# Halved convolution operations, re-timed norm broadcasts and an end that accumulates onto the old sum, in a hybrid decoder step

## The chip, the core and the metric

The kernel runs on one core of one Trainium2 chip. The metric is the device time of one execution in microseconds (us). The core's engines are named as the profile names them: PE (TensorE, matrix products), PEld (its weight loads), DVE (VectorE), ACT (ScalarE), POOL (GpSimd) and SP (SyncE, which here only issues transfers). Matrix products write into PSUM, a small memory of eight banks; everything else that is on the chip lies in SBUF. Each engine works through its own queue in order, and waits on semaphores for the others.

## The reference

One inference step of a one-layer hybrid decoder: sliding-window attention and a state-space mixer side by side, then a squared-ReLU MLP and a last norm. 1024 prompt tokens (plus 16 meta tokens) and 32 sample tokens go through it in fp32. What matters here:

```python
def causal_conv(x, prev, conv_w, conv_b):
    t = x.shape[1]
    xp = jnp.concatenate([prev, x], axis=1)
    y = sum((xp[:, j:j + t] * conv_w[j] for j in range(CONV_W)), conv_b)      # CONV_W = 4
    return jax.nn.silu(y), xp[:, t:]

def rmsnorm(x, g):
    xf = x.astype(jnp.float32)
    y = xf * lax.rsqrt(jnp.mean(xf * xf, axis=-1, keepdims=True) + EPS)
    return (y * g.astype(jnp.float32)).astype(x.dtype)

def mix_and_mlp(h, ao, so, attn_out_g, w_out, norm2_g, w_up, w_down):
    mix = jnp.concatenate([rmsnorm(ao, attn_out_g), so], axis=-1)             # ao: attention's output
    h = h + mix @ w_out
    u = jax.nn.relu(rmsnorm(h, norm2_g) @ w_up)
    return h + (u * u) @ w_down
...
    y_prompt = rmsnorm(hp, norm_f_g)[:, N_META:]
    y_sample = rmsnorm(hs, norm_f_g)
```

## The kernel before

Channels lie on the 128 partitions and tokens along the free axis. Each fp32 product is done as three matrix products of a high and a low part (`three`, or `whi`, `wlo`, `acth`, `actl` in the names). All matrix products but the transposes are issued by the helper `mm` at line 202, so the profile gives them line 202 and only their tiles tell them apart.

**Attention and convolution** (about 100 to 300 us into the span). `interleave` walks through slots. The generator `projections` gives one slot per input projection: 24 matrix products into a bank `g`, 304 or 384 columns wide. At the head of each slot every live chain is advanced by one step. The chains are nine attention tiles, of which tile i (1 to 8) starts in slot 24 + round(3.3 (i - 1)), that is 24, 27, 31, 34, 37, 40, 44, 47. Counted from its start S, a tile (`attn_block`) prepares its operands `kS` and `Qs` in slot S, makes scores (bank `s`) and the softmax `p` in S+1 and S+2, transposes `p` into banks `pt` (line 743) and copies them out as `pT` (line 745) in S+3 and S+4, and multiplies by the values (bank `o`) in S+5. `norm_o` then norms the tile: squares `sqo`, their sum over channels by a matrix product `o<-ones,sqo` in S+7, the root `rsb` (DVE line 320, then POOL line 321), a diagonal `dg` (ACT line 376), a broadcast by the matrix product `pt<-dg,ones`, and a multiplication (DVE, line 762) that reads the bank. There are two `pt` buffers. The broadcast stands in slot S+9 for tiles 1 to 7, since `late` is true for them, and in S+8 for tiles 0 and 8.

The convolution (`conv`) runs under the same slots, one group m of 128 channels after the other: ACT makes the first tap (line 522), DVE the other three (line 524, each 128x1096 in and out of the same tile `acc`, named `xs` or `bc`), ACT a tanh (line 529), DVE the last product (line 531). POOL shares the stage: it splits weights (`wlo`, line 234) and scales the softmax (`p`, line 733). The order of the instructions within a queue is set when the program is built, by a scheduler that may move them past each other, so the code's order alone does not tell it.

**The end.** The output has four parts of TQ = 264 tokens. The last loop (`last`) adds one more product to part 0 (16 steps of four channel groups), then to groups 0, 1 and 2 of part 1 (16 steps), then to group 3 of part 1 (16 steps). After each group DVE adds the bank to `h` (line 1801). `final_last` is the norm of part 1. It sums the squares of seven groups ahead, while group 3 is still being multiplied (`c<-ones,ac`), then squares group 3 (line 1756), sums it over channels for three token tiles, takes the root (lines 1762 and 1763), builds three diagonals (line 1654), broadcasts (`c<-dg,ones`), multiplies `h` on DVE in four pieces (line 1665), and stores each (line 1768), on SP's and ACT's queues in turn. Six idle products into a bank `g` keep PE busy while the root is taken.

Of the kernel before, what the change touches and what calls it, by code (L numbers as in the profile page):

```python
# [15 lines left out]
D = 1024  # L16
# [152 lines left out]
_OUTS = [('y', (128, 4, 8, TQ)), ('kp', (128, 128)), ('vp', (128, 128)), ('cv_', (128, 8, 27)), ('hp', (128, 512)),  # L169
# [22 lines left out]
def body(ctx: ExitStack, tc: tile.TileContext, xT, xm, win, wdt, wo, wu, wd, ck, cv, sc, st, sT, vec, consts,  # L192
# [323 lines left out]
    def conv(m, cb):  # L516
        acc = (xs if m < 4 else bc[0])[:, m % 4, :]
        cw_ = lambda j: vec[:, V_CW + 8 * j + m:V_CW + 8 * j + m + 1]
        seq = cb[:, 0:56].rearrange("p (b t) -> p b t", t=7)
# [3 lines left out]
        for j in range(1, 4):  # L523
            DVE.scalar_tensor_tensor(out=acc, in0=cb[:, j:j + CL], scalar=cw_(j), in1=acc, op0=ALU.mult, op1=ALU.add)  # L524
            if j > 1:
                yield
# [4 lines left out]
        DVE.scalar_tensor_tensor(out=acc, in0=th, scalar=1.0, in1=acc, op0=ALU.add, op1=ALU.mult)  # L531
# [223 lines left out]

    def norm_o(i, o_ps=None):
# [4 lines left out]
        ps = yield from rms_bcast(pa, POOL, ps_tile, sq[:, :, :rows], rows, 512, "o", "pt", late=0 < i < NT - 1)  # L761
# [106 lines left out]
    for q in range(4):  # L868
# [16 lines left out]
               [(24 + round(3.3 * (i - 1)), attn_block(i)) for i in range(1, NT)])  # L885
# [731 lines left out]
    sums2 = {}  # L1617

    def squared(c, n):

        hc = h[:, n:n + 4, two(c)]
        q2 = hpool.tile([128, 4, TQ], F32, name="q2", tag="q2", bufs=2)
# [7 lines left out]
        else:  # L1630
            sums2[c] = hpool.tile([128, TQ], F32, name=f"ac{c}")
# [7 lines left out]
    def gained(c, m):  # L1639
        hm = h[:, m, two(c)]  # L1640
        ACT.activation(out=hm, in_=hm, func=AF.Copy, scale=vec[:, V_GF + m:V_GF + m + 1])

    AT = (0, 128, TQ - 128)

    def sum_tokens(tag, acc):
        pt = bank(tag)
        for q, a in enumerate(AT):
            mm(pt[:, q:q + 1], acc[:, a:a + 128], ones[:, 0:1], True, True)
        return pt
# [7 lines left out]
    def spread(tag, dgs):  # L1657
        ps = bank(tag)
        for a, dg in zip(AT, dgs):
# [3 lines left out]
    def normed(c, ps, m, n):  # L1663
        hm = h[:, m:m + n, two(c)]
        DVE.tensor_tensor(out=hm, in0=hm, in1=ps[:, :TQ].unsqueeze(1).broadcast_to([128, n, TQ]), op=ALU.mult)

    def final(c, tag, waits):

        yield from squared(c, 0)
        pt = sum_tokens(tag, sums2[c])  # L1670
# [33 lines left out]
    for i, (j, k) in enumerate(down):  # L1704
# [32 lines left out]
    kept2 = [w2p.tile([128, 2, TQ], F32R, name=f"tk{k}") for k in range(16)]  # L1737

    def final_last():

        hc = h[:, :, two(1)]
        q2 = hpool.tile([128, 4, TQ], F32, name="q2", tag="q2", bufs=2)
# [7 lines left out]
        pt = sum_tokens("c", sums2[1])  # L1750
# [3 lines left out]
        DVE.tensor_scalar(out=part, in0=pt[:, 0:3], scalar1=1.0 / D, scalar2=EPS, op0=ALU.mult, op1=ALU.add)  # L1754
        yield
        ACT.activation(out=q2[:, 3], in_=hc[:, 3], func=AF.Square)
        pt = sum_tokens("c", q2[:, 3])
# [3 lines left out]
        rs = hpool.tile([128, 3], F32, name="rs3", tag="rs3", bufs=2)  # L1761
        DVE.scalar_tensor_tensor(out=rs, in0=pt[:, 0:3], scalar=1.0 / D, in1=part, op0=ALU.mult, op1=ALU.add)
        POOL.tensor_tensor(out=rs, in0=rs, in1=nhalf[:, 0:3], op=ALU.pow)
        gained(1, 3)
        ps = spread("c", [diag(rs, q) for q in range(3)])
# [65 lines left out]
```

## Time and profile before

| what | value |
|---|---|
| median of 3 runs | 1129.44 us (1129.01 to 1130.55) |
| the profiled execution's own time | 1129.86 us |
| its span, from the first to the last instruction | 1128.1 us |
| what lies around the span | 1.76 us |
| busy in the span: PE, PEld | 1110.9 us (98%), 1072.0 us (95%) |
| busy in the span: DVE, ACT, POOL | 838.4 us (74%), 569.9 us (51%), 220.8 us (20%) |
| granted TensorE clock | 0.999 |

A busy PE is not a PE at its peak: matrix products are pipelined, and the ends of them are modelled. The shares are averages over stages with different limits, so each part of the change is to be judged in its own stage.

### The profile page before, as it was taken

To read this page: it belongs to the slowest core of one execution; us is meant where nothing else is said; L and a number is where in the kernel's file an instruction comes from. 1 tells how busy PE (TensorE), PEld (TensorE's weight loads), DVE (VectorE), ACT (ScalarE), POOL (GpSimd) and SP (SyncE) were. 2 spreads that over 40 slices of the span, in tenths; PEclk is the share of its full clock that TensorE was granted. 3 is DMA by queue.
4 is the path that set the end of the run, shared out by engine and by line. 5 is a ranking of instruction groups with operands and counts; after the bars stand their busy time and mean duration, and the time that the engine had idled before them with its cause. 6 is when DMAs were issued, how large, how long until landed. Compare 5 with 4: busy or idle time off the path is not lost.

```text
span 1128.1 us, 21788 instructions
## 1 busy us (share of the span) xinstructions
PE 1110.9 (98%) x8405; PEld 1072.0 (95%) x8405; DVE 838.4 (74%) x1627; ACT 569.9 (51%) x1203; POOL 220.8 (20%) x290
## 2 busy tenths in 40 slices
PE   9999999999999999999999999999999999999997
PEld 8989989889888899999999999999999999999996
DVE  6646888885788968998877767766599656778483
ACT  8312467575666648854444444444434334546461
POOL 0442365664343442210000000000000000000010
PEclk9999999999999999999999999999999999999999
DMA  8131110111466476666652433525989653465272
GB/s 291 66 98 38 38 27 31 38 53 42 157 199 211 130 273 211 214 184 224 208 187 106 168 147 134 180 89 182 383 302 321 192 174 102 125 199 163 77 237 99
DMA packets 84424, 177.64 MB, mean 157 GB/s; under 512 B 10692, under 2 KB 32740, under 8 KB 82272
## 3 DMA queue, kind: packets, MB, share of 16 engines
q1 hardware_dynamic: 77392, 141.58, 40.3%
q0 software_dynamic: 6224, 33.74, 7.5%
q8 instruction: 66, 1.08, 0.4%
q10 hardware_dynamic: 704, 0.93, 0.2%
q14 instruction: 38, 0.31, 0.1%
HBM read 125.49 MB, written 50.72 MB: 156 GB/s over the span
## 4 chain that ended last, share of the span: by engine, by line
PE 80%; DVE 9%; ACT 5%; issue 3%; DMA 2%; POOL 0%; POOLq 0%; DVEq 0%; ACTq 0%
PE g L202 43%; PE b L202 19%; PE c L202 9%; PE s L202 3%; PE o L202 1%; ACT p L679 1%; PE y L202 1%; DMA wdr<-in_wd 1%; PE pt L743 1%; DVE Qs L710 1%; DVE bc L524 1%; DVE Sd L1600 1%; DVE p L677 1%; ACT acth L407 1%; PE pt L202 1%
## 5 line engine op out<-in xcount | busy, mean ns | idle before, releaser
L202 PE MATMUL g<-acth,whi 128*128 128x384 f32 (+2 forms) x528 | 161.8, 331 | 0.2 <-DVE qT L454 0.2
L202 PE MATMUL g<-acth,wlo 128*128 128x384 f32 (+2 forms) x528 | 159.4, 327 | 0.4 <-DVE hb L985 0.4
L202 PE MATMUL g<-actl,whi 128*128 128x384 f32 (+2 forms) x432 | 140.6, 326 | 0.0
L1613 ACT CAST ts<-tr 128x528 fp32r<-128x528 f32 x92 | 58.3, 634 | 118.7 <-PE b L202 100.1
L1614 DVE TENSOR_TENSOR ts<-tr,ts 128x528 fp32r<-128x528 f32 x92 | 65.1, 708 | 53.1 <-ACT ts L1613 52.7
L202 PEld LDWEIGHTS g<-acth,whi 128*128 128x128 f32 x528 | 97.2, 188 | 2.0 <-issue 1.0
L202 PEld LDWEIGHTS g<-acth,wlo 128*128 128x128 f32 x528 | 97.1, 188 | 0.9 <-DVE hb L985 0.6
L202 PEld LDWEIGHTS g<-actl,whi 128*128 128x128 f32 x432 | 81.4, 188 | 0.1
L321 POOL TENSOR_TENSOR rs<-rs,nhalf 128x3 f32<-128x3 f32 x9 | 10.6, 1181 | 333.5 <-DMA wdq<-in_wd 285.3
L1329 ACT COPY s<-g 128x264 f32<-128x264 f32 x90 | 33.8, 377 | 61.0 <-PE g L202 61.0
L234 POOL TENSOR_TENSOR wlo<-wraw,whi 128x256 fp32r<-128x256 f32 x56 | 48.9, 904 | 12.5 <-ACT whi L231 12.3
L1402 POOL DMA_DIRECT2D u<-u x16 | 8.5, 533 | 175.8 <-ACT u L1345 146.7
L1334 DVE TENSOR_TENSOR u<-b,s 128x264 f32<-128x264 f32 x64 | 27.5, 430 | 19.5 <-PE b L202 10.1
L733 POOL TENSOR_TENSOR p<-p,sm 128x512 f32<-128x512 f32 (+1 forms) x32 | 35.3, 1126 | 31.7 <-DVE sm L731 29.9
L1339 ACT ACTIVATE u<-u 128x528 f32<-128x528 f32 x42 | 27.2, 648 | 27.0 <-DVE u L1338 27.0
L202 PE MATMUL b<-ts,w7y 128*128 128x264 f32 x279 | 39.3, 285 | 0.0
L202 PE MATMUL g<-ts,whi 128*128 128x264 f32 x279 | 38.9, 284 | 0.0
L202 PE MATMUL g<-ts,w7y 128*128 128x264 f32 x279 | 38.9, 283 | 0.0
L202 PE MATMUL b<-ts,whi 128*128 128x264 f32 x279 | 38.9, 284 | 0.0
L202 PE MATMUL g<-ts,wlo 128*128 128x264 f32 x270 | 38.0, 285 | 0.0
L202 PE MATMUL b<-ts,wlo 128*128 128x264 f32 x270 | 37.3, 282 | 0.0
L679 ACT ACTIVATE p<-p,nm 128x257 f32<-128x257 f32 (+1 forms) x64 | 31.4, 493 | 10.6 <-DVE nm L677 10.4
(578 smaller groups left out, 3476.3 us busy)
## 6 DMA issues: line engine op xcount, KB each, us to landing
tr<-u SPq DMA_DIRECT2D x92, 264.0 KB, 3.2
wraw<-in_wu SPq DMA_DIRECT2D x38, 512.0 KB, 4.0
wdr<-in_wd SPq DMA_DIRECT2D x68, 256.0 KB, 3.9
u<-t POOLq DMA_DIRECT2D x16, 1056.0 KB, 5.7
wraw<-in_win SPq DMA_DIRECT2D x16, 512.0 KB, 3.7
u<-u POOLq DMA_DIRECT2D x10, 792.0 KB, 3.6
wraw<-in_wo SPq DMA_DIRECT2D x24, 256.0 KB, 2.9
h<-he SPq DMA_DIRECT2D x16, 264.0 KB, 4.9
```

The source lines that it names most:

```text
L202: PE.matmul(out, lhsT=a, rhs=b, start=start, stop=stop, skip_group_check=on)
L234: eng.tensor_tensor(out=lo[:, n], in0=raw[:, n], in1=f(hi[:, n]), op=ALU.subtract)
L407: ACT.activation(out=hk, in_=xt[:, n], func=AF.Copy, scale=g)
L524: DVE.scalar_tensor_tensor(out=acc, in0=cb[:, j:j + CL], scalar=cw_(j), in1=acc, op0=ALU.mult, op1=ALU.add)
L677: DVE.tensor_tensor_reduce(out=s_out[:, 0:W], in0=ps, in1=mask, scale=-scale, scalar=nsink, op0=ALU.add, op1=ALU.min, accum_out=nm)
L679: ACT.activation(out=s_out[:, 0:W + 1], in_=s_out[:, 0:W + 1], func=AF.Exp, bias=nm, scale=-1.0, accum_out=sm)
L733: POOL.tensor_tensor(out=p[:rows, r:r + 2, :W], in0=p[:rows, r:r + 2, :W], in1=sm[:rows, r:r + 2].unsqueeze(2).broadcast_to([rows, 2, W]), ...
L1329: ACT.copy(out=s[:, c], in_=ps[c][:, :TQ])
L1334: DVE.tensor_tensor(out=out[:, c], in0=ps[c][:, :TQ], in1=s[:, c], op=ALU.add)
L1339: ACT.activation(out=x, in_=x, func=AF.Square)
L1613: ACT.copy(out=t[:, 0], in_=x)
L1614: DVE.tensor_tensor(out=t[:, 1], in0=x, in1=f(t[:, 0]), op=ALU.subtract)
```

## The change

It has three parts.

1. `conv`: each of the four DVE operations on a 128x1096 tile becomes two on 128x548. That is 8 x 4 = 32 DVE instructions more.
2. `late_of(i)` replaces `late`: the broadcast of tile i goes to the first slot from S+8 on in which no tile has its transposes. Tiles 0 and 8 stay in S+8. For tiles 1, 3, 4, 5 and 7 that is S+8, one slot earlier than before, for tiles 2 and 6 it is S+9, as before. (The few words of the change, "later for two of the tiles", are against S+8 for all.)
3. The end: the four parts become 272, 256, 264 and 264 tokens wide (`LASTQ`), so that the last one to finish, part 1, has two token tiles and not three. The output's layout follows. Group 3 of part 1 is no longer added by DVE: ACT copies the old `h` into the bank `ps3` at step 28 of the loop, four steps ahead of group 3's first product, and the products accumulate onto it. Square and gain of that group then read the bank. The broadcast is made in two banks (`c` and `g`); ACT copies the second to SBUF (`fk`), and POOL multiplies two of the eight channel groups with it while DVE does the six others.

```diff
     def conv(m, cb):
+        halves = ((0, CL // 2), (CL // 2, CL))
         ACT.activation(out=acc, in_=cb[:, 0:CL], func=AF.Identity, scale=cw_(0), bias=vec[:, V_CB + m:V_CB + m + 1])
         for j in range(1, 4):
-            DVE.scalar_tensor_tensor(out=acc, in0=cb[:, j:j + CL], scalar=cw_(j), in1=acc, op0=ALU.mult, op1=ALU.add)
+            for a, b in halves:
+                DVE.scalar_tensor_tensor(out=acc[:, a:b], in0=cb[:, j + a:j + b], scalar=cw_(j), in1=acc[:, a:b], op0=ALU.mult, op1=ALU.add)
...
-        DVE.scalar_tensor_tensor(out=acc, in0=th, scalar=1.0, in1=acc, op0=ALU.add, op1=ALU.mult)
+        for a, b in halves:
+            DVE.scalar_tensor_tensor(out=acc[:, a:b], in0=th[:, a:b], scalar=1.0, in1=acc[:, a:b], op0=ALU.add, op1=ALU.mult)
...
+    START = [0] + [24 + round(3.3 * (i - 1)) for i in range(1, NT)]
+    def late_of(i):
+        if i == 0 or i == NT - 1:
+            return 0
+        taken = {START[n] + q for n in range(1, NT) for q in (3, 4)}
+        return next(n for n in range(9) if START[i] + 8 + n not in taken)
...
-        ps = yield from rms_bcast(pa, POOL, ps_tile, sq[:, :, :rows], rows, 512, "o", "pt", late=0 < i < NT - 1)
+        ps = yield from rms_bcast(pa, POOL, ps_tile, sq[:, :, :rows], rows, 512, "o", "pt", late=late_of(i))
...
+LASTQ = ((0, 272), (272, 256), (528, 264), (792, 264))
...
     def final_last():
...
-        ACT.activation(out=q2[:, 3], in_=hc[:, 3], func=AF.Square)
-        pt = sum_tokens("c", q2[:, 3])
+        ACT.activation(out=q2[:, 3], in_=ps[3][:, :w], func=AF.Square)
+        pt = sum_tokens("c", q2[:, 3], 1)
         for _ in range(6):
             mm(idle2[:, 0:128], q2[:, 3, 0:128], ones, True, True)
...
-        gained(1, 3)
-        ps = spread("c", [diag(rs, q) for q in range(3)])
-        for m, n, q in ((4, 2, SP), (6, 2, ACT), (0, 3, SP), (3, 1, ACT)):
-            normed(1, ps, m, n)
-            q.dma_start(out=y[:, 1, m:m + n], in_=hc[:, m:m + n])
+        ACT.activation(out=hc[:, 3], in_=ps[3][:, :w], func=AF.Copy, scale=vec[:, V_GF + 3:V_GF + 4])
+        dgs = [diag(rs, q) for q in range(nt)]
+        fac, fac2 = spread("c", dgs, 1), spread("g", dgs, 1)
+        kept = hpool.tile([128, LW], F32, name="fk")
+        ACT.copy(out=kept[:, :w], in_=fac2[:, :w])
+        normed(1, fac, 4, 2)
+        normed(1, kept, 6, 2, POOL)
+        store(SP, 1, 4, 2)
+        normed(1, fac, 0, 3)
+        store(SP, 1, 0, 3)
+        normed(1, fac, 3, 1)
+        store(ACT, 1, 6, 2)
+        store(ACT, 1, 3, 1)
...
+        if i == 28:
+            ps3 = bank("g")
+            ACT.copy(out=ps3[:, :width(1)], in_=h[:, 3, part_(1)])
...
+        onto = c == 1 and ms == (3,)
         for m in ms:
             for n, (a, b) in enumerate(three):
-                mm(ps[m][:, :TQ], w2[k][:, a, m, :], t[:, b], k == 0 and n == 0, k == 15 and n == 2)
-            if k == 15:
+                mm(ps[m][:, :width(c)], w2[k][:, a, m, :], t[:, b], not onto and k == 0 and n == 0, k == 15 and n == 2, onto)
+            if k == 15 and not onto:
```

The rows that follow show how the built program's queues change, at three places. A row is a line, an operation, the output's tile and the inputs' tiles, and the shape; "x4" is four such instructions in a row. Lines 524, 531, 646, 731, 745, 762 of before are lines 528, 536, 651, 736, 750, 776 of the changed kernel.

First, PE around the broadcast of tile 3, before; `o` and `s` are steps of younger tiles, `g` a projection:

```order
L202 MATMUL g<-acth_124,wlo 128x384
L202 MATMUL o<-pT,vt 64x512 x4
L202 MATMUL s<-kS,Qs 128x256 x8
L202 MATMUL g<-acth_115,whi 128x304
...
L202 MATMUL g<-acth_116,wlo 128x304
L202 MATMUL pt<-dg,ones 128x128
L743 MATMUL pt<-cs,p 128x128 x4
```

The same place of the changed kernel:

```order
L204 MATMUL g<-acth_124,wlo 128x384
L204 MATMUL pt<-dg,ones 128x128
L204 MATMUL o<-pT,vt 64x512 x4
L204 MATMUL s<-kS,Qs 128x256 x8
L204 MATMUL g<-acth_115,whi 128x304
...
L748 MATMUL pt<-cs,p 128x128 x8
```

The broadcast moved ahead of a whole projection, and the eight transposes, which were four and, some products later, four more, stand together.

Second, DVE's queue around the second convolution tap of group m = 6, before; each L677 pair is one softmax row block, and four such pairs stand ahead of this piece:

```order
L524 SCALAR_TENSOR_TENSOR bc<-cb,vec,bc 128x1096
L646 TENSOR_TENSOR cb<-g,rb_133 128x8x4
L731 RECIPROCAL sm<-sm 128x4
L445 TENSOR_TENSOR cb<-g,rb_133 128x272
L762 TENSOR_TENSOR qT<-qT,pt 128x4x128
L745 COPY pT<-pt 128x512
```

The same place of the changed kernel, of which the first row of line 528 is the first tap's second half and the second tap's first half:

```order
L528 SCALAR_TENSOR_TENSOR bc<-cb,vec,bc 128x548 x2
L736 RECIPROCAL sm<-sm 128x4
L528 SCALAR_TENSOR_TENSOR bc<-cb,vec,bc 128x548
L651 TENSOR_TENSOR cb<-g,rb_133 128x8x4
L447 TENSOR_TENSOR cb<-g,rb_133 128x272
L750 COPY pT<-pt 128x512
```

The multiplication of the norm (line 762, now 776) left this place for one ahead of the first tap, the softmax's pairs moved ahead of the first tap's second half, and the reciprocal between two halves.

Third, DVE's last rows, before:

```order
L1801 TENSOR_TENSOR h<-h,b 128x264
L1762 SCALAR_TENSOR_TENSOR rs_13468<-c,rp_13436 128x3
L1654 TENSOR_SCALAR dg_13472<-cs,rs_13468 128x128
L1654 TENSOR_SCALAR dg_13474<-cs,rs_13468 128x128
L1654 TENSOR_SCALAR dg_13476<-cs,rs_13468 128x128
L1665 TENSOR_TENSOR h<-h,c 128x2x264 x2
L1665 TENSOR_TENSOR h<-h,c 128x3x264
L1665 TENSOR_TENSOR h<-h,c 128x264
```

And of the changed kernel:

```order
L1785 SCALAR_TENSOR_TENSOR rs_13498<-c,rp_13468 128x2
L1670 TENSOR_SCALAR dg_13502<-cs,rs_13498 128x128
L1670 TENSOR_SCALAR dg_13504<-cs,rs_13498 128x128
L1686 TENSOR_TENSOR h<-h,c 128x2x256
L1686 TENSOR_TENSOR h<-h,c 128x3x256
L1686 TENSOR_TENSOR h<-h,c 128x256
```

The last addition, one diagonal and one of the four multiplications are gone from DVE's queue.

More of the change, by code (lines that the diff above doesn't have):

```diff
@@ L884, in body @@
     interleave(projections(), [(13, step_chain()), (16, first())] +
-               [(24 + round(3.3 * (i - 1)), attn_block(i)) for i in range(1, NT)])
+               [(START[i], attn_block(i)) for i in range(1, NT)])
     SP.dma_start(out=cv_, in_=tail)
@@ L1617, in body @@
     sums2 = {}
+    part_ = lambda c: slice(LASTQ[c][0], sum(LASTQ[c]))
+    width = lambda c: LASTQ[c][1]
+    starts = lambda c: [min(a, width(c) - 128) for a in range(0, width(c), 128)]
+    LW = max(w for _, w in LASTQ)
     def squared(c, n):
-        hc = h[:, n:n + 4, two(c)]
-        q2 = hpool.tile([128, 4, TQ], F32, name="q2", tag="q2", bufs=2)
+        hc = h[:, n:n + 4, part_(c)]
+        q2 = hpool.tile([128, 4, LW], F32, name="q2", tag="q2", bufs=2)[:, :, :width(c)]
         ACT.activation(out=q2, in_=hc, func=AF.Square)
@@ L1639, in gained, with sum_tokens @@
     def gained(c, m):
-        hm = h[:, m, two(c)]
+        hm = h[:, m, part_(c)]
         ACT.activation(out=hm, in_=hm, func=AF.Copy, scale=vec[:, V_GF + m:V_GF + m + 1])
-    AT = (0, 128, TQ - 128)
-    def sum_tokens(tag, acc):
+    def sum_tokens(tag, acc, c):
         pt = bank(tag)
-        for q, a in enumerate(AT):
+        for q, a in enumerate(starts(c)):
             mm(pt[:, q:q + 1], acc[:, a:a + 128], ones[:, 0:1], True, True)
@@ L1655, in diag, with spread, store, normed @@
         return dg
-    def spread(tag, dgs):
+    def spread(tag, dgs, c):
         ps = bank(tag)
-        for a, dg in zip(AT, dgs):
+        for a, dg in zip(starts(c), dgs):
             mm(ps[:, a:a + 128], ones, dg, True, True)
         return ps
-    def normed(c, ps, m, n):
-        hm = h[:, m:m + n, two(c)]
-        DVE.tensor_tensor(out=hm, in0=hm, in1=ps[:, :TQ].unsqueeze(1).broadcast_to([128, n, TQ]), op=ALU.mult)
+    def store(q, c, m, n):
+        a, w = LASTQ[c]
+        q.dma_start(out=y[:, 8 * a + m * w:8 * a + (m + n) * w].rearrange("p (m t) -> p m t", m=n), in_=h[:, m:m + n, part_(c)])
+    def normed(c, ps, m, n, eng=DVE):
+        w = width(c)
+        hm = h[:, m:m + n, part_(c)]
+        eng.tensor_tensor(out=hm, in0=hm, in1=ps[:, :w].unsqueeze(1).broadcast_to([128, n, w]), op=ALU.mult)
     def final(c, tag, waits):
         yield from squared(c, 0)
-        pt = sum_tokens(tag, sums2[c])
+        pt = sum_tokens(tag, sums2[c], c)
+        n = len(starts(c))
         for _ in range(waits[0]):
@@ L1684, in final @@
             normed(c, ps, m, 2)
-            SP.dma_start(out=y[:, c, m:m + 2], in_=h[:, m:m + 2, two(c)])
+            store(SP, c, m, 2)
             yield
@@ L1736, in body @@
     w2p = ctx.enter_context(pool("w2p", side="right"))
-    kept2 = [w2p.tile([128, 2, TQ], F32R, name=f"tk{k}") for k in range(16)]
+    kept2 = [w2p.tile([128, 2, width(1)], F32R, name=f"tk{k}") for k in range(16)]
     def final_last():
-        hc = h[:, :, two(1)]
-        q2 = hpool.tile([128, 4, TQ], F32, name="q2", tag="q2", bufs=2)
+        hc, w = h[:, :, part_(1)], width(1)
+        nt = len(starts(1))
+        q2 = hpool.tile([128, 4, LW], F32, name="q2", tag="q2", bufs=2)[:, :, :w]
         ACT.activation(out=q2[:, 0:3], in_=hc[:, 0:3], func=AF.Square)
```

40 lines of the change are left out of this document (20 added, 20 removed).

## The prediction

> **What bounds the kernel now.** I read the waits of PE first, because a kernel whose PE is 98% busy can only become faster where PE stands still, or after PE's last product. Then the same waits of DVE in two stretches, the busy times of the stages, and the order of time at each place that the change touches. PE's and PEld's waits between 100 and 300 us, the stage of attention and convolution (what waited, for what, us in total, times, longest):
>
> ```profile
> PE pt L743 <- DVE qT L762: 1.8, 2, 1.1
> PE pt L743 <- ACT pT L745: 0.5, 1, 0.5
> PE pt L743 <- DVE pT L745: 0.4, 1, 0.4
> PE pt L202 <- ACT dg L376: 0.2, 1, 0.2
> ...
> PEld pt L743 <- DVE qT L762: 2.4, 2, 1.4
> ```
>
> In 200 us PE stands for 2.9 us, and 1.8 us of it are two waits of transposes for the norm's multiplication. PEld stands longer in them, 2.4 us, since the modelled end of a product hides a part. The busy times of four stretches (length, then PE, PEld, DVE, ACT, POOL with instruction counts, clock, DMA):
>
> ```profile
> 176.00:246.00 70.00, 68.19 (x446) 62.61 (x446) 63.13 (x134) 46.53 (x118) 43.53 (x52) 1.00 0.12 37
> 246.00:300.00 54.00, 53.84 (x342) 48.53 (x341) 31.20 (x88) 30.93 (x82) 24.11 (x34) 1.00 0.19 59
> 1063.00:1110.00 47.00, 47.00 (x392) 47.00 (x391) 37.00 (x87) 25.51 (x55) 3.14 (x3) 1.00 0.55 171
> 1110.00:1129.00 19.00, 10.05 (x80) 9.41 (x79) 5.98 (x15) 3.14 (x6) 0.85 (x1) 0.89 0.27 90
> ```
>
> The down projection (third row) is full of PE work: nothing beside it counts. In the last row PE works half of the time: that is the end, a chain of single steps. The first two rows differ in DVE: 63 of 70 us, then 31 of 54. DVE's waits in 176 to 246 us, and behind the dots in 246 to 300 us:
>
> ```profile
> DVE bc L524 <- ACT bc L522: 4.0, 3, 1.5
> DVE sm L731 <- ACT p L679: 1.9, 5, 0.5
> DVE cb L445 <- PE g L202: 1.2, 1, 1.2
> ...
> DVE g L445 <- PE g L202: 12.4, 7, 3.5
> ```
>
> From 176 to 246 us DVE waits for PE once, at the start; for the rest it is busy or waits for ACT. There DVE with ACT sets the pace and PE runs ahead of it, standing where it gets too far. After 246 us DVE waits for PE seven times, so a lag of DVE is made good there.
>
> **The change part by part.** The sum is made against the profiled execution, 1129.86 us (span 1128.1, 1.76 around it), which is 0.42 us above the median.
>
> *The broadcasts.* One of the two waits, in order of time:
>
> ```profile
> 215.68 1.76 DVE L524 SCALAR_TENSOR_TENSOR bc<-cb,vec,bc 128x1096 f32<-128x1096 f32 x1
> 215.78 0.38 PE L202 MATMUL pt<-dg,ones 128*128 128x128 f32 x2
> 216.00 0.60 PE L743 MATMUL pt<-cs,p 128*128 128x128 f32 x4
> 218.16 0.68 DVE L762 TENSOR_TENSOR qT<-qT,pt 128x512 f32<-128x512 f32 x1
> 218.89 0.66 PE L743 MATMUL pt<-cs,p 128*128 128x128 f32 x4 [1.07 <-DVE qT L762]
> ```
>
> The broadcast takes one `pt` buffer, the first four transposes the other; the second four wait until line 762 has read the first, and line 762 stands behind a 1.76 us convolution operation. The new order puts the broadcast a projection (some 4 us) earlier and line 762 ahead of the first tap, so at the transposes both buffers are free. The same goes for tile 4. This takes off 1.8 to 2.4 us; I take the middle, **-2.1 us**, since the modelled ends hide part of PE's wait. What is late next is DVE's copy of `pT` (line 745), needed by the transposes a slot later: it was queued behind line 762 and gains its 0.68 us, then loses to the halves. Tiles 5 and 7 move where DVE has room: nothing.
>
> Tile 1 is tight. Its diagonal chain before:
>
> ```profile
> 166.89 0.14 DVE L320 TENSOR_SCALAR rsb<-o 128x1 f32<-128x1 f32 x1
> 167.23 0.56 POOL L321 TENSOR_TENSOR rsb<-rsb,nhalf 128x1 f32<-128x1 f32 x1
> 167.83 0.41 ACT L376 ACTIVATE dg<-cs,rsb 128x128 f32<-128x128 f32 x1 [2.55 <-POOL rsb L321]
> 168.61 0.65 PE L202 MATMUL o<-pT,vt 128*64 128x512 f32 x2
> ```
>
> The diagonal is ready at 168.24; the broadcast now stands in front of the product at 168.61. That leaves 0.37 us, and line 320 is queued behind four halves now. If they delay it by about 0.7, PE waits 0.3. Bounds 0 and 1.0; I take **+0.3 us**, near the row's own slack.
>
> *The halves.* Costs of DVE operations:
>
> ```profile
> L524 DVE SCALAR_TENSOR_TENSOR bc<-cb,vec,bc 128x1096 f32<-128x1096 f32 x12 | 18.7, 1558 | 4.1 <-ACT bc L522 4.0
> 185.54 1.36 DVE L524 SCALAR_TENSOR_TENSOR bc<-cb,vec,bc 128x1096 f32<-128x1096 f32 x1
> 1092.65 0.70 DVE L1625 TENSOR_TENSOR q<-q 128x528 f32<-128x528 f32 x1
> 1101.83 0.43 DVE L1700 TENSOR_TENSOR tk<-trq,tk 128x264 fp32r<-128x264 f32 x1 [0.97 <-ACT tk L1699]
> 1099.00 0.77 DVE L1700 TENSOR_TENSOR tk<-trq,tk 128x264 fp32r<-128x264 f32 x2
> 214.15 3.88 POOL L234 TENSOR_TENSOR wlo<-wraw,whi 128x256 fp32r<-128x256 f32 x4
> 219.35 1.04 POOL L733 TENSOR_TENSOR p<-p,sm 128x512 f32<-128x512 f32 x1
> ```
>
> 264 columns more cost 0.70 - 0.43 = 0.27 us, so a lone operation has 0.16 us that do not scale. Two that do not depend on each other take 0.77, so the second adds 0.34, of which 0.07 is fixed. Two halves are independent, so 0.07 is the nearer price: 32 x 0.07 = 2.2 us of DVE, 1.1 of them in 176 to 246 us, where 16 of the 32 operations run. By the lone price it is 5.1 and 2.6 us.
>
> [...]
>
> Besides, the 1.76 us operation against the free 1.36: it stood 0.40 us while POOL's weight split ran, as the mean of 1.558 over twelve says of many. A POOL operation that has begun makes DVE wait, and the other way round; a second half may wait once more. [...] The mean wait is 1.56 - 1.36 = 0.2 us an operation, and with twice as many starts it is at most paid twice: 24 x 0.2 = 4.8 us more of DVE (the last product's eight are mostly free of it), half in 176 to 246 us. What DVE loses, POOL gains.
>
> Against it stand the gains of the finer order: the softmax's rows, which stood behind a whole operation, stand behind its first half (0.65 us sooner), and the reciprocal, which waited 1.9 us in all for ACT's exponentials, finds a half in front of it. So in the stretch that DVE bounds there is +1.1 to +5.0 (2.6 and 2.4) on one side and at least 1.9 on the other, and PE's remaining waits in the stage (0.9 us, for `pT`) are, with tile 1's 0.3, the most that can come back. On PE's time I take **0**, with -1.2 and +3 as ends; the cover is DVE's idle time after 246 us, and where that is gone each us on DVE is one on the end.
>
> *Widths.* Part 0 has 192 products eight columns wider, part 1 has 192 eight narrower: 0.
>
> *The end.* The chain before, from group 3's last steps:
>
> ```profile
> 1113.12 0.74 PEld L202 LDWEIGHTS c<-ones,ac 128*128 128x128 f32 x6
> 1116.90 0.43 DVE L1801 TENSOR_TENSOR h<-h,b 128x264 f32<-128x264 f32 x1 [2.75 <-PE b L202]
> 1117.37 0.42 ACT L1756 ACTIVATE q<-h 128x264 f32<-128x264 f32 x1 [4.39 <-DVE h L1801]
> 1117.84 0.74 PEld L202 LDWEIGHTS c<-ones,q 128*128 128x128 f32 x6 [1.19 <-ACT q L1756]
> 1118.53 1.58 PE L202 MATMUL g<-ones,q 128*128 128x128 f32 x12
> 1119.01 0.85 POOL L1763 TENSOR_TENSOR rs<-rs,nhalf 128x3 f32<-128x3 f32 x1 [18.88 <-DVE rs L1762]
> 1120.30 0.74 PEld L202 LDWEIGHTS c<-dg,ones 128*128 128x128 f32 x6 [0.38 <-PE g L202]
> 1121.28 2.21 DVE L1665 TENSOR_TENSOR h<-h,c 128x528 f32<-128x528 f32 x3 [0.70 <-PE c L202]
> ...
> GB/s 0 0 0 0 0 0 0 0 0 0 0 0 0 0 0 0 0 38 353 315 377 369 315 338 376 346 357 357 356 46 12 8 0 0 0 0 0 0 0 0
> DMA packets 1089, 1.09 MB, mean 99 GB/s; under 512 B 64, under 2 KB 1088, under 8 KB 1088
> ```
>
> - No addition: the square starts where the addition started, 1117.37 - 1116.90: **-0.47**.
> - The sum has four passes and not six, each 0.74 / 6 = 0.12: **-0.25**; the same for the sum inside group 3's products (first row): **-0.25**.
> - The root of two columns: 0.85 for three here, 0.56 for one (tile 1's row), so 0.15 a column: **-0.15**. The idle products (1.58) leave PE as much earlier.
> - The broadcast has four passes ahead of DVE: **-0.25**. The four of the second bank come behind it.
> - The multiplications: DVE loses two channel groups of eight, about 0.6 us, to POOL. But the last two rows (1118 to 1129 us in 40 slices of 0.28) show eleven slices at some 350 GB/s: from the first store on the DMA engines are full, and 1.09 MB takes them 3 us. The first store leaves behind the first multiplication, as before. Bytes shrink by 8 of 264 columns (-0.1), and the second store now waits for three groups and not two (+0.1): **0**. POOL's path, second broadcast 0.5, copy 0.4, product 1.04 (line 733's row, the same size), is done some 2 us in, before the engines run dry; were POOL as slow as in the shared stretches, +0.4.
>
> The end sums to -1.4 us (bounds -0.9 and -1.7). With -2.1 + 0.3: **-3.2 us**, 1126.7 in the profiled execution's terms, 1126.2 in the median's.
>
> **The rivals.**
> - *The stage gives nothing back.* DVE is the bound from 176 to 246 us; PE, no longer held at `pt`, meets DVE at `Qs` or `pT` a slot later. For it: 63 of 70 us busy. Against it: DVE's idle time right behind. Only the end is left: 1129.44 - 1.4 = 1128.0.
> [...]
> - *The finer order pays.* The waits for `pT` (0.9) go as well, and tile 1 costs nothing: -3.2 - 1.2, so 1125.0. For it: the softmax starts 0.65 us earlier per block.
> - *Slower: POOL gets between the halves.* In 176 to 246 us each second half of 16 lets one more POOL operation of 0.4 (the measured wait) pass, 6.4 us, and the fixed cost is 2.6; less 1.9 of filled waits, 7.1 on the bound: -3.2 + 7.1, so 1133.3. It decides from 5.5 us on DVE (3.2 + 0.2%). Against it: POOL is busy 43.5 of 70 us, not always, and finishes earlier for it.
>
> **How the numbers follow.** 0.2% of 1129.44 is 2.26 us, about what a measurement here can tell from no change: faster is below 1127.2. Chances: my sum 0.44 (its own range 1125.4 to 1127.3), the finer order 0.20, nothing back 0.22, the lone price 0.08, slower 0.06. Faster is the first two less a little at the sum's upper edge, and a small part of the third if the end gives 1.7 and more: 0.64. Same 0.30, slower 0.06. For 8 in 10 the range reaches from below the finer order, 1124.4, to just above the lone price, 1128.9.
>
> **What would show it.** Right: no wait of line 743's transposes for the norm's multiplication; DVE's busy time up by 2 to 5 us; line 1801 gone from the last chain and the first store some 1.4 us earlier against the last group's start; stores still back to back. Wrong: new waits of PE for `Qs`, `kS` or `pT` between 176 and 246 us, a wait of tile 1's broadcast over 1 us, DVE still without waits for PE after 246 us, or a last store that waits for POOL.

## The result, and the profile after

The changed kernel takes 1132.45 us (median of 22 runs, 1130.27 to 1135.72), the kernel before, run beside it, 1130.06 (22 runs). The ratio is 1.0020, with a 95% interval of 1.0015 to 1.0026: some 2.3 us slower, where the prediction had 3.2 us faster. It lies outside the range.

The profiled execution took 1133.61 us, its span is 1131.8. Four stretches, bounded by rows that both kernels have, share the 3.76 us between the two spans (start to tile 0's sum `o<-ones,sqo`; to tile 8's; to the first `c<-ones,ac`; to the end; us):

| stretch | before | after | difference |
|---|---|---|---|
| start | 124.10 | 126.24 | +2.14 |
| attention and convolution | 171.83 | 173.82 | +1.99 |
| middle | 801.84 | 802.64 | +0.80 |
| end | 30.31 | 29.14 | -1.17 |

PE's waits between 100 and 300 us, in the profile after (what waited, for what, us in total, times, longest):

```profile
PE pt L204 <- ACT dg L378: 1.2, 2, 1.0
PE pt L748 <- DVE pT L750: 1.2, 2, 0.9
PE pt L748 <- ACT pT L750: 1.0, 2, 0.5
PE s L204 <- DVE Qs L715: 0.3, 1, 0.3
```

The waits for the norm's multiplication, 1.8 us before, are gone as predicted, and 0.9 us of waits for the copies `pT` have become 2.2, with 1.2 for diagonals where 0.2 was. The stage's two later stretches:

```profile
176.00:246.00 70.00, 69.71 (x453) 64.50 (x453) 64.73 (x154) 47.04 (x124) 43.01 (x56) 1.00 0.10 33
246.00:300.00 54.00, 53.01 (x334) 48.09 (x333) 33.32 (x91) 31.05 (x82) 21.91 (x27) 1.00 0.18 57
```

Where DVE was to be the bound (first row), PE is now fuller than before, 69.71 of 70 us and not 68.19. Counted between the tiles' sums `o<-ones,sqo`, the stage lost 2.04 us up to tile 2's (184.41 us), won 1.48 up to tile 5's (243.81), where the two old waits stood, and lost 1.43 behind that, where PE is less full than before (second row: 53.01 of 54 us and not 53.84). The convolution's taps in DVE's groups after (shape, count, then busy time and mean ns of one):

```profile
L528 DVE SCALAR_TENSOR_TENSOR bc<-cb,vec,bc 128x548 f32<-128x548 f32 x24 | 24.3, 1038 | 2.4 <-ACT bc L525 2.3
L528 DVE SCALAR_TENSOR_TENSOR xs<-cb,vec,xs 128x548 f32<-128x548 f32 x24 | 21.3, 936 | 3.2 <-ACT xs L525 3.1
```

And before, for the groups in `xs` (those in `bc`, 18.7 us, stand in the prediction):

```profile
L524 DVE SCALAR_TENSOR_TENSOR xs<-cb,vec,xs 128x1096 f32<-128x1096 f32 x12 | 18.9, 1571 | 3.2 <-ACT xs L522 3.1
```

The 24 taps took 37.6 us whole and take 45.6 in halves, 0.33 us more a tap: 0.20 in `xs`, the groups 0 to 3, and 0.47 in `bc`, the groups 4 to 7. (The halves overlap a little, so their busy time is less than count times mean: 24.3 us in `bc`, against 24 x 1.038 = 24.9.)

The start is code that the change does not touch. The window from 20 to 25 us before (the number ahead of the last two is the granted clock):

```profile
20.00:25.00 5.00, 4.95 (x33) 4.95 (x34) 5.00 (x11) 5.00 (x11) 0.20 (x1) 1.00 0.86 273
```

And after:

```profile
20.00:25.00 5.00, 4.71 (x21) 4.47 (x22) 4.92 (x9) 5.00 (x10) 0.00 (x0) 0.66 0.77 267
```

PE did 21 products in these 5 us and not 33: the clock fell to 0.50 (so from 22 to 24 us, where before had 1.00), after PE had waited 0.96 us, and not 0.60, for the fourth weights.

The end, in order of time:

```profile
1121.20 0.38 ACT L1779 ACTIVATE q<-g 128x256 f32<-128x256 f32 x1 [3.53 <-PE g L204]
1121.64 0.52 PEld L204 LDWEIGHTS c<-ones,q 128*128 128x128 f32 x4 [0.68 <-ACT q L1779]
1122.59 0.70 POOL L1786 TENSOR_TENSOR rs<-rs,nhalf 128x2 f32<-128x2 f32 x1 [17.50 <-DVE rs L1785]
1124.47 1.88 DVE L1686 TENSOR_TENSOR h<-h,c 128x512 f32<-128x512 f32 x3 [0.67 <-PE c L204]
1124.92 0.37 ACT L1792 COPY fk<-g 128x256 f32<-128x256 f32 x1 [2.97 <-PE g L204]
1125.37 1.26 POOL L1686 TENSOR_TENSOR h<-h,fk 128x512 f32<-128x512 f32 x1 [2.09 <-ACT fk L1792]
1126.66 0.96 ACTq L1681 DMA_DIRECT2D out_y<-h  x2
```

The square follows PE at once, the sum has four passes, the root takes 0.70 and not 0.85, all as predicted. But from the first multiplication to the end of the span it is 1131.84 - 1124.47 = 7.37 us, where before it was 1128.08 - 1121.28 = 6.80. ACT's two stores are issued only at 1126.66, behind POOL's multiplication.

### The profile page after: what moved, and what is told of

Read it like the earlier page. It is cut to its first block, busy times and chain, and to the rows that moved or that the text cites. A ratio compares the mean times of both kernels' runs of the same rounds, so it can differ in the third digit from the quotient of the medians.

```text
span 1131.8 us, 21829 instructions
## 1 busy us (share of the span) xinstructions
PE 1113.0 (98%) x8403; PEld 1073.8 (95%) x8403; DVE 843.9 (75%) x1656; ACT 569.3 (50%) x1205; POOL 216.5 (19%) x291
## 4 chain that ended last, share of the span: by engine, by line
PE 84%; DVE 8%; ACT 3%; issue 2%; DMA 2%; POOL 0%; POOLq 0%; SPq 0%; ACTq 0%; DVEq 0%
PE g L204 46%; PE b L204 19%; PE c L204 9%; PE s L204 4%; PE o L204 2%; PE pt L204 1%; PE pt L748 1%; PE y L204 1%; DVE xs L528 1%; DVE Sd L1614 1%; DMA wraw<-in_win 1%; DVE wdr L1622 1%; DVE ts L1628 1%; PE f L204 1%; DVE Qs L715 0%
## 5 line engine op out<-in xcount | busy, mean ns | idle before, releaser
L236 POOL TENSOR_TENSOR wlo<-wraw,whi 128x256 fp32r<-128x256 f32 x56 | 45.3, 837 | 11.4 <-ACT whi L233 11.3
```

What stands on the lines that cost most here:

```text
L236: eng.tensor_tensor(out=lo[:, n], in0=raw[:, n], in1=f(hi[:, n]), op=ALU.subtract)
```

## The experiments

All times are against the kernel before on the same chip. "Stage" is the length from tile 0's to tile 8's sum against 171.83 us before, "end" that from the first `c<-ones,ac`, against 30.31.

| run | median, us (before) | ratio, 95% interval | stage | end |
|---|---|---|---|---|
| halves alone | 1132.96 (1130.39) | 1.0021, 1.0011 to 1.0031 | +3.32 | -0.05 |
| broadcasts alone | 1130.06 (1130.39) | 0.9996, 0.9985 to 1.0006 | -0.03 | +0.02 |
| end alone | 1129.17 (1130.39) | 0.9987, 0.9977 to 0.9996 | -0.09 | -1.19 |
| changed kernel, idle products at the start | 1132.09 (1130.39) | 1.0008, 0.9998 to 1.0017 | +1.96 | -1.18 |
| end, DVE alone | 1128.26 (1129.98) | 0.9980, 0.9969 to 0.9992 | -0.07 | -1.96 |
| broadcasts, ACT scales a part of p | 1127.56 (1129.98) | 0.9974, 0.9962 to 0.9986 | -2.38 | -0.03 |
| quiet POOL, whole | 1126.47 (1129.98) | 0.9964, 0.9952 to 0.9976 | -3.43 | -0.36 |
| quiet POOL, halves | 1126.50 (1129.98) | 0.9965, 0.9954 to 0.9977 | -3.72 | -0.33 |
| changed kernel, taps whole | 1129.21 (1129.81) | 0.9998, 0.9990 to 1.0007 | 0.00 | -1.19 |
| fast kernel | 1126.28 (1129.81) | 0.9964, 0.9951 to 0.9978 | -2.37 | -1.96 |
| fast, idle products | 1126.25 (1129.81) | 0.9966, 0.9954 to 0.9979 | -2.12 | -1.97 |
| fast, all halves | 1128.89 (1129.81) | 0.9989, 0.9980 to 0.9998 | -0.11 | -1.95 |
| fast, halves in groups 4 to 7 | 1127.03 (1130.57) | 0.9968, 0.9956 to 0.9981 | -2.17 | -1.97 |
| fast, halves in groups 0 to 3 | 1129.64 (1130.57) | 0.9990, 0.9979 to 1.0002 | -0.09 | -1.96 |

In the runs with "quiet POOL", POOL's two large tasks are left out. The "fast kernel" has the moved broadcasts, ACT's scaling of a part of `p`, the new end with DVE alone, and whole convolution operations.

The lengths of stage and end repeat within some 0.3 us for the same code from one execution to another, and so tell more than the medians. The start (123.4 to 126.3 us) and the middle (800.9 to 803.6) scatter by 3 us, in code that the edits hardly touch.

### The three parts by themselves

Halves: only the two loops over `halves` in `conv`.

> The kernel before with the halved convolution operations alone. Theory A (the halves are what cost: each second half lets one more POOL operation in, DVE is the bound from 130 to 250 us): 2 to 4 us slower than before, with alternating POOL and DVE rows in the stage and new waits of PE for pT, Qs or a diagonal between 140 and 300 us. Rival B (the halves cost nothing on PE, and the moved broadcasts brought the new waits): within 0.5 us of before. Rival C (only the clock at the start differs between runs): no difference between runs of equal granted clock.

The time is as theory A had it, 1.2 to 3.5 us slower; that DVE's total work is the bound doesn't follow from it (see below). In the profile, which is of the slowest of the eleven runs, what it costs PE has three places. Two stand ahead of 171 us (below). The third is the old wait for line 762 (765 here), now 2.3 us long, and what follows it:

```profile
PE pt L746 <- DVE qT L765: 2.3, 1, 2.3
```

DVE's rows there, in order of time:

```profile
219.86 2.21 DVE L526 SCALAR_TENSOR_TENSOR bc<-cb,vec,bc 128x548 f32<-128x548 f32 x2
222.08 0.89 DVE L526 SCALAR_TENSOR_TENSOR bc<-cb,vec,bc 128x548 f32<-128x548 f32 x1
223.34 0.67 DVE L765 TENSOR_TENSOR qT<-qT,pt 128x512 f32<-128x512 f32 x1
```

And the window behind it:

```profile
225.00:229.00 4.00, 4.00 (x17) 4.00 (x16) 3.30 (x7) 1.19 (x3) 0.07 (x1) 0.57 0.00 0
```

Three halves (3.1 us) stand ahead of the multiplication where one whole operation (1.76 us) stood. Behind the wait the clock is 0.57 for 4 us, which takes 4 x 0.43 = 1.7 us of full clock: here the wait of 2.3 us cost PE over 1.5 us a second time. In the changed kernel this place is empty, since the moved broadcasts take the multiplication out of it.

Broadcasts: only `late_of`.

> The kernel before with the moved broadcasts alone. Theory A: the two waits of transposes for the norm's multiplication vanish and little comes in their place, since line 320 of tile 5 again follows its sum by some 2.5 us: 1.5 to 2 us faster than before. Rival B: tile 1's and tile 5's broadcasts now wait for their diagonals by 0.4 and about 1.2 us and the copies pT come as late as they did: 0 to 0.5 us faster, or up to 1 us slower.

Theory A falls, and so does the mechanism of B: the stage is as long as before, but neither a diagonal nor a copy took the time. Among PE's waits is a new one:

```profile
PE pt L743 <- POOL p L733: 1.5, 3, 0.6
```

One of its three places, in order of time:

```profile
220.32 2.62 POOL L733 TENSOR_TENSOR p<-p,sm 128x512 f32<-128x512 f32 x2
222.12 0.41 PE L743 MATMUL pt<-cs,p 128*128 128x128 f32 x2
223.00 0.88 PE L743 MATMUL pt<-cs,p 128*128 128x128 f32 x6 [0.46 <-POOL p L733]
```

From the start of one product to the start of the next, PE took 1.23 and 0.91 us longer at the two old waits than between products that don't wait (its pitch), 2.14 in all. Now it stands 0.62, 0.62, 0.13 and 0.77 us at three slots, again 2.14: the transposes of a tile's second group reach POOL's scaling of `p` by that much too early.

End: part widths, old sum in the bank, POOL's multiplication.

> The kernel before with the new end alone (part widths, old sum in the bank, POOL's multiplication). Theory A: first store 1.1 us earlier, 0.6 us of it lost again between the first multiplication and the end, where the span waits for POOL's drain: 0.5 us faster than before. Rival (the drain hides behind the stores and the loss was chance): 1.1 to 1.4 us faster. Rival C: the program's length or layout makes the halved clock at 21 to 25 us more frequent: mean granted clock .996 to .997 in over half of the runs, and no faster than before.

The end is 1.19 us shorter (ratio: 0.5 to 2.6 us faster), so the size that theory A gave was too small, though the 0.57 us behind the first multiplication were lost here too (1127.05 - 1119.69 = 7.36). Four of the eleven runs have a mean clock of .997 or less, and the median is below that of before, which speaks against C.

### The start's clock

```diff
                 psq.append(gps())
+                if ch == 0:
+                    for _ in range(8):
+                        mm(psq[1][:, :cw], w0[2][0][:, 0, :], X[ch][0][0][:, 0, :], True, True)
```

> The changed kernel with eight idle products (128x304, 0.14 us each, 1.1 us in all) ahead of the first product with the fourth weights, where PE waited 1.5 us before its clock fell to half. Theory D (that wait at 18.6 to 20.1 us brings the halved clock of 21 to 25 us, which some runs have and others not): every run shows a granted clock of .998 or more, and the median falls by 1 to 1.5 us against the changed kernel, to about 1131.2. Rival (the clock falls for another reason, such as the waits at 7 and 9 us): the same two groups of runs as before, .996 to .997 and .998 to .999, about 2 us apart.

```profile
20.00:25.00 5.00, 5.00 (x36) 5.00 (x35) 5.00 (x11) 5.00 (x11) 0.17 (x1) 1.00 0.87 285
```

The clock is whole, tile 0's sum is at 124.15 us and not 126.24, and ten of eleven runs have a mean clock of .998 or more: for the clock, theory D holds. For the time it isn't settled. The ratio falls from 1.0020 to 1.0008, that is by some 1.4 us, and the intervals of the two overlap only from 1.0015 to 1.0017; but the median falls by 0.4 us alone, to 1132.09 and not to 1131.2, while the nine runs of the changed kernel with a clock of .998 or more have a median of 1131.16. Before the edit, 13 of the changed kernel's 22 runs lay at .997 or less, and 16 of the 33 of the kernel before beside this run, so a fall in the clock isn't shown to depend on the change. In the changed kernel's profile ACT's cast of the fourth weights waited 0.89 us for their load and began at 19.43 us, before at 18.66. The wait's length alone doesn't decide it: the clock fell after 1.04, 1.21 and 1.60 us from start to start, and stood after 1.19 and 1.20 in two other profiles.

### POOL at the end

```diff
-        fac, fac2 = spread("c", dgs, 1), spread("g", dgs, 1)
...
+        fac = spread("c", dgs, 1)
+        for m, n, q in ((4, 2, SP), (6, 2, ACT), (0, 3, SP), (3, 1, ACT)):
+            normed(1, fac, m, n)
+            store(q, 1, m, n)
```

> The kernel before with the new end, but without POOL's part of it: one broadcast, DVE makes all four multiplications, stores on SP's and ACT's queues in turn as before. Theory A (the 0.57 us that the stretch from the first multiplication to the end grew, 7.37 after 6.80, comes from POOL's multiplication and the late stores behind it): that stretch is 6.6 to 6.8 us again, and the kernel is about 0.6 us faster than with the new end as it stands, 1.7 us faster than before. Rival (the stretch is set by the transfers' own time, which the narrower part or the new layout changed): 7.3 us as with POOL, 1.1 us faster than before.

```profile
1119.26 2.48 DVE L1683 TENSOR_TENSOR h<-h,c 128x512 f32<-128x512 f32 x4 [0.67 <-PE c L204]
1119.97 1.83 SPq L1678 DMA_DIRECT2D out_y<-h  x2
1120.57 1.56 ACTq L1678 DMA_DIRECT2D out_y<-h  x2
```

ACT's first store leaves 1.3 us behind the first multiplication's start, and not 2.2. The stretch is 1125.85 - 1119.26 = 6.59 us, and the end 1.96 us shorter than before. The size is theory A's: POOL's two groups cost some 0.8 us. Of its two reasons the late stores count for little: the last packet ends 5.21 us behind the first multiplication's start, 5.29 with POOL, 5.36 before. The rest lies between the last packet and the end of the span (see the last section). The edit also takes out the second broadcast and ACT's copy, and changes the order of the stores; no run parts these from POOL's multiplication.

### POOL's scaling as the next wait

In tiles 4, 5 and 6, second group, ACT scales two of the four rows of `p`:

```diff
             for r in range(0, 4, 2):
+                if r and g and i in (4, 5, 6):
+                    for rr in (2, 3):
+                        ACT.activation(out=p[:rows, rr, :W], in_=p[:rows, rr, :W], func=AF.Copy, scale=sm[:rows, rr:rr + 1])
+                    continue
                 POOL.tensor_tensor(out=p[:rows, r:r + 2, :W], ...
```

> The kernel before with the moved broadcasts, and in tiles 4, 5 and 6 two of the four rows of the second group's softmax are scaled by ACT (line 735) and not by POOL. Theory A (the 2.1 us that PE no longer waits for the norm's multiplication went into waits of the transposes for POOL's scaling of p, 0.6 to 0.9 each at 204, 222 and 241 us): those three waits fall below 0.2 each, and the stage from 124 to 300 us is 1.5 to 2 us shorter than with the moved broadcasts alone, which gained nothing; 1.5 to 2 us faster than before. Rival (another step, the copies pT or Qs, is late at the same moment again): 0 to 0.5 us faster than before.

```profile
PE pt L747 <- ACT pT L749: 0.5, 1, 0.5
PE pt L747 <- DVE pT L749: 0.4, 1, 0.4
PE pt L202 <- ACT dg L376: 0.2, 1, 0.2
```

What is left is what before had beside the two large waits. The stage is 2.38 us shorter, the kernel 1.6 to 4.3 us faster. Theory A holds: the two moves together are worth what the prediction gave the broadcasts alone. No run has ACT's scaling without the moved broadcasts, so what the scaling would bring by itself isn't shown.

### What a half costs, and where

Without POOL's weight splits and its scaling (left out; the high parts stand in for the low ones), whole and halved:

> The kernel before without POOL's two large tasks in the stage: the low parts of the weights of this stage are left out (the high part is used in their place) and the softmax is not scaled. For reading against the next run. Theory A (DVE's whole operations are stretched by POOL): line 524 has a mean of 1.36 to 1.40 us and not 1.60. Rival (the stretch has another cause): 1.55 to 1.6.

> The same as the run before it, with the halved convolution operations. Theory A (what a half costs beside half of a whole is POOL's doing): the halves of the taps have a mean of 0.70 to 0.75 us and not 0.95 to 0.99, DVE's busy time grows by no more than 1.5 us against the whole operations, and the two kernels differ by less than 0.5 us. Rival (each half pays a fixed price of 0.16 us or more): the mean is 0.84 or more, DVE's busy time grows by 5 us, and the kernel is 1 to 3 us slower than with whole operations.

The taps in `bc`, whole:

```profile
L525 DVE SCALAR_TENSOR_TENSOR bc<-cb,vec,bc 128x1096 f32<-128x1096 f32 x12 | 16.3, 1355 | 4.9 <-ACT bc L523 4.8
```

And halved:

```profile
L527 DVE SCALAR_TENSOR_TENSOR bc<-cb,vec,bc 128x548 f32<-128x548 f32 x24 | 18.1, 782 | 4.9 <-ACT bc L524 4.8
```

A whole tap takes 1.355 us, 1.558 with POOL; the stretching by POOL is confirmed. Twelve taps take 1.8 us more in halves, 0.15 a tap: nearly the lone price of 0.16, not the 0.07 that I took. With POOL it was 0.47, so of the price in `bc` POOL makes two thirds. Theory A was too low on DVE (a mean of 0.782 and not 0.70 to 0.75, DVE's busy time up by 3.9 us and not 1.5, which is nearer the rival's 5), and right on the time: the two kernels are equal, and the stage is 0.29 us shorter with halves. Here the fixed price costs PE nothing; whether the finer order pays isn't shown, since 0.29 us is no more than the stage's own scatter.

Then the parts put together:

> The changed kernel with the convolution's operations whole again: moved broadcasts and the new end are left. Theory A (the parts add: broadcasts nothing, end 1.2 us): about 1.2 us faster than before, and 2 to 3.5 us faster than the changed kernel, which is the price of the halves inside it. Rival (the halves cost so much only where the broadcasts stay, as in the run with the halves alone, and the changed kernel's loss comes from tiles 1 and 5): 0 to 1 us faster than the changed kernel, so no faster than before.

> Moved broadcasts, ACT's scaling of two softmax rows in tiles 4 to 6, the new end with DVE alone, whole convolution operations. Theory A (stage and end add): 2.4 and 1.8 us off, about 4.2 us faster than before, near 1126. Rival (one eats the other, or both gains were chance): 2.5 us or less.

> The same as the run before it, with six idle products (0.14 us each) ahead of the first product with the fourth weights. Theory D (PE's wait there costs a second time by the clock, in the runs in which it is long): nearly no run with a clock under .998, the median 0.3 to 1 us below the kernel without them. Rival (the products cost as much in the runs with a short wait as they save in the others): the same median within 0.3 us, with less spread.

> The kernel two runs before (moved broadcasts, ACT's scaling, the end with DVE alone) with the halved convolution operations. Theory A (the halves cost by what POOL puts between them, and POOL still splits the weights): 1.5 to 3 us slower than with whole operations. Rival (with POOL's scaling out of the chain, the finer order pays as it did with POOL quiet, 0.4 us of the stage): the same within 0.5 us, or faster.

With whole taps the changed kernel's stage is as long as before and its end 1.19 us shorter; by the ratio it lies between 1.1 us faster and 0.8 slower than before, and some 2.5 us (0.0022) below the changed kernel. This last is theory A's price of the halves; its 1.2 us faster than before lies just outside the interval. The fast kernel gains 2.5 to 5.5 us; the parts add (2.4 and 2.0). Idle products change nothing there: the rival. Halves in the fast kernel cost 2.8 us (0.9989 against 0.9964), of which the stage shows 2.26; the middle of these two profiles differs by another 1.8, of which more below. The last two runs say where:

> The fast kernel (moved broadcasts, ACT's scaling in tiles 4 to 6, the end with DVE alone) with the convolution's operations halved in groups 4 to 7 alone, which run after some 176 us. Theory A (the 2.0 us of PE's new waits in the fully halved kernel all stand between 144 and 171 us, under the groups 1 to 3; where DVE is busiest, from 176 to 246 us, the halves cost PE nothing once tile 5's broadcast and p have room): no wait over 0.2 us there beyond those of the kernel with whole operations, the same time as that within 0.5 us. Rival (halves cost where DVE is busiest, as the prediction had it): 1.5 to 3 us slower.

> The same with the operations halved in groups 0 to 3 alone. Theory A: the waits of transposes at about 144, 146, 163 and 164 us and of tile 1's broadcast at 170 us stand as in the fully halved kernel (1.1, 0.5 more than with whole operations, and 0.4 us), and the kernel is 2 to 2.6 us slower than with whole operations. Rival: the same time as with whole operations within 0.5 us.

PE's waits in the run with groups 0 to 3 halved:

```profile
PE pt L752 <- DVE pT L754: 1.2, 2, 0.9
PE pt L752 <- ACT pT L754: 1.0, 2, 0.5
PE pt L204 <- ACT dg L378: 0.4, 2, 0.2
```

And the taps of groups 4 to 7 in the fast kernel:

```profile
L526 DVE SCALAR_TENSOR_TENSOR bc<-cb,vec,bc 128x1096 f32<-128x1096 f32 x12 | 18.6, 1551 | 2.9 <-ACT bc L524 2.8
```

And in the run with groups 4 to 7 halved:

```profile
L528 DVE SCALAR_TENSOR_TENSOR bc<-cb,vec,bc 128x548 f32<-128x548 f32 x24 | 24.4, 1042 | 2.4 <-ACT bc L525 2.3
```

Theory A holds at both ends. In groups 4 to 7 the taps take 24.4 us and not 18.6, 5.8 us more, in the part of the stage where DVE is busiest, and the stage grows by 0.20. In groups 0 to 3 they take 21.3 and not 18.8, less than half of that, and the stage grows by 2.28, at 144 to 171 us. DVE's whole busy time between the two sums grows alike in both, from 133.8 us to 135.9 and to 136.5: in groups 4 to 7 other operations give back what the taps take. So not the amount of DVE's work decides. In groups 0 to 3 the mechanism is one of order. The first of the three places there, in the kernel before, in order of time:

```profile
139.28 0.62 ACT L709 CAST Qs<-qT 64x512 fp32r<-64x512 f32 x1
139.94 0.68 DVE L710 TENSOR_TENSOR Qs<-qT,Qs 64x512 fp32r<-64x512 f32 x1 [0.38 <-ACT Qs L709]
141.06 1.96 POOL L733 TENSOR_TENSOR p<-p,sm 128x352 f32<-128x352 f32 x2 [3.86 <-DVE sm L731]
141.45 0.93 DVE L710 TENSOR_TENSOR Qs<-qT,Qs 64x512 fp32r<-64x512 f32 x1 [0.46 <-ACT Qs L709]
142.89 0.67 DVE L745 COPY pT<-pt 48x512 f32<-48x512 f32 x1
```

And in the changed kernel:

```profile
142.73 1.24 ACT L714 CAST Qs<-qT 64x512 fp32r<-64x512 f32 x2
143.11 1.95 POOL L738 TENSOR_TENSOR p<-p,sm 128x352 f32<-128x352 f32 x2 [2.84 <-DVE sm L736]
143.36 2.25 DVE L715 TENSOR_TENSOR Qs<-qT,Qs 64x512 fp32r<-64x512 f32 x2 [0.33 <-ACT Qs L714]
146.12 0.67 DVE L750 COPY pT<-pt 48x512 f32<-48x512 f32 x1
146.94 0.60 PE L748 MATMUL pt<-cs,p 128*48 128x128 f32 x4 [0.26 <-DVE pT L750]
```

Before, ACT's first cast of tile 2's `Qs` stood ahead of the last exponentials, and DVE's first subtraction was done before POOL began to scale `p`. With halves the built program has both casts behind the exponentials; both subtractions start inside POOL's scaling and take 2.25 us, against 0.68 + 0.93 before, and `pT` comes 3.2 us later, of which the start accounts for 2.1. All profiles with halves in groups 0 to 3 and POOL at work have this order and the 2.25 us; the fast kernel and the run with groups 4 to 7 halved have the old order and 0.69 + 0.93. With POOL quiet the halves have the new order too, the two take 1.40, and PE doesn't wait. So at this place, 1.1 of the 2.0 us, it is where POOL's work falls among DVE's that counts. The two other places (0.5 and 0.4 us) aren't taken apart here, and no run has halves with the old order. In the kernel before, single rows of either engine are longer while the other works: DVE's first subtraction of `kS` (line 692) took 0.28 us at 228.48, with POOL idle, and 1.07 at 219.47, inside POOL's scaling of 219.35 to 221.44; POOL's copy `tail` of 128x3 (line 521), 0.19 us in the median of eight, took 1.26 at 231.87, begun 0.16 us after a tap of 1.37.

## Why the prediction was wrong

The stage took 1.99 us more, where the sum had 1.8 less (-2.1 + 0.3 + 0), and the end 1.17 less, where it had 1.4.

- *The broadcasts, -2.1.* The two waits went, as predicted; the step that failed is "what is late next is DVE's copy of `pT`". It was POOL's scaling of `p` (line 733), which had been hidden behind the longer wait and took the whole 2.14 us back. The rival "the stage gives nothing back" had this outcome, with `Qs` or `pT` as its cause.
- *Tile 1, +0.3.* PE stood 0.39 us longer than its pitch at 172 us, in the changed kernel: right.
- *"Tiles 5 and 7 move where DVE has room: nothing."* Wrong for tile 5. Before, line 320 followed its sum after 2.5 us (241.11 to 243.61). In the changed kernel it followed after 5.3 (243.81 to 249.10), the diagonal was ready at 250.31, and PE stood 1.16 us at the broadcast:

```profile
249.10 0.15 DVE L322 TENSOR_SCALAR rsb<-o 128x1 f32<-128x1 f32 x1
250.37 0.49 PE L204 MATMUL pt<-dg,ones 128*128 128x128 f32 x2 [0.99 <-ACT dg L378]
```

With broadcasts alone line 320 followed after 4.5 us and the diagonal was ready 0.5 us ahead of PE, so most of the delay came with the broadcasts and left little room. With ACT's scaling it followed after 3.6 us, and no wait is seen there either.

- *The halves, 0.* DVE's busy time from 120 to 300 us grew from 139.5 to 145.4 us, of which the broadcasts alone bring 2.3 (141.7); the rest is within the 2.2 to 7 of the working, and DVE's idle time behind 246 us did cover what happened in 176 to 246 us. The step that failed is where the price was looked for: it was bounded for the stretch in which DVE is busiest, and PE paid 2.0 us at 144 to 171 us, where DVE has idle time but a chain of short steps passes through DVE and POOL in turn. The slower rival's mechanism (POOL gets between the halves) was real, with 5.6 us more for the taps of groups 4 to 7, and cost PE 0.2 there: a half in `bc` took 0.26 us longer with POOL at work than with it quiet (1.038 and 0.782), where the prediction had 0.2 at most. What DVE lost POOL gained in part: in the changed kernel its weight splits took a mean of 0.837 us, and not 0.904. The lone price was real too, and cost nothing with POOL quiet. That sixteen halves at the lone price, 2.6 us of DVE, come out in the time one for one, as the range's upper edge and the chance of 0.08 have it, no run shows: with POOL quiet DVE's busy time grew by 3.9 us and the two kernels were equal.
- *The end, -1.4.* Measured -1.17 to -1.19: near it, by luck, since two misses offset each other. The chain up to the first multiplication gained 1.75 us and not 1.37. Behind group 3's last product the terms held (1.11 us, 1.12 in the sum); ahead of it 0.64 came off and not 0.25, for which group 3's narrower products may count in part (the sum had 0 for widths). The multiplications, taken as 0 with +0.4 as the bound, were mis-sized: +0.57 against the old end, +0.78 against DVE alone at the new width. That the transfers would hide POOL's path was right, though ACT's stores waited for POOL: the last packet ended 5.29 us behind the first multiplication's start, 5.36 before. What grew is the way from the last packet to the end of the span (below), for which the sum had no term.
- *Not in the prediction:* the granted clock (0.66 from 20 to 25 us). 2.1 us of the profile's difference, and part of the medians', come from the start, where no instruction was changed.

What stays open is the middle, in which profiles differ by up to 2.7 us, in short waits at other places each time. Eight profiles with whole operations and POOL at work have 800.9 to 802.7 us there, 801.7 in the mean; the six with halves in some or all groups have 802.5 to 803.3, 802.9 in the mean. So the halves may cost up to 1.2 us there too. One execution of each doesn't settle it, and no run here settles the cause. The quiet pair has it the other way (803.6 whole, 801.5 halved), but in the whole one the clock fell to half at 303 us for 3.41 us, which accounts for most of that. The +0.80 us of the changed kernel lies within that scatter.

## What to carry to other kernels

A wait in the list names only the last of several late steps: before a step is moved to end a wait, look for what else the waiting instruction needs, and when that is ready; here the second one took the whole gain back, and moving both was worth 2.4 us. The share of busy time doesn't tell where an added cost lands: with halves in groups 4 to 7, DVE's 2.1 us more in the stage cost 0.2 us; with halves in groups 0 to 3, where DVE is looser, its 2.7 us more cost 2.3, since they came with a new order in a chain of short steps. Here the split of an operation on DVE gave POOL another place to enter, 0.47 us a tap in `bc` against 0.15 with POOL quiet, and with the last of the work on POOL the end of the span stood 2.08 us behind the last packet, and not 1.44.

## What the runs showed of the hardware

- The end of the span follows the last output packet by 2.08 us where POOL multiplied last (packets until 1129.76, span until 1131.84), and by 1.44 us where it didn't (1126.64, 1128.08); with DVE alone at the new width, 1.38. All four profiles with POOL's multiplication have 2.07 or 2.08, the twelve others 1.37 to 1.53. POOL's `DRAIN` at the program's end took 5.72 us from 1125.3 in the changed kernel, so to 1131.0, when SP's first had begun at 1130.3; before it took 5.29 from 1119.0, so to 1124.3, and SP's first began at 1127.3.
- Ahead of the kernel's end the clock fell to half (0.50 from 22 to 24 us in the changed kernel) behind waits of 1.0 to 2.6 us from start to start, and once, in the quiet kernel with whole operations at 303 us, behind waits of no more than 0.8, and stayed there for 3.41 us each time. In the traces' record of the clock, the stretches between two such changes are whole numbers of 3.41 us: 17.07 is 5 of them (changed kernel), 13.65 is 4 and 201.39 is 59 (halves alone), 296.96 is 87 (quiet, whole). Waits of about 1.2 us came out both ways: with the changed kernel's taps whole, one of 1.20 us left the clock alone, while the clock fell behind one of 1.21 in the changed kernel, and behind one of 1.04 with groups 4 to 7 halved. What decides it isn't shown.
